# Level masks on GpSimd alone, the first loads spread over three queues, and one gate column later in the fill

## The chip, the cores and the metric

One core of a Trainium2 chip runs the kernel. Its engines are TensorE (PE in the profile, with its weight loads as PEld), VectorE (DVE), ScalarE (ACT), GpSimd (POOL) and SyncE (SP); each works through its own instructions in order. SP, ACT and POOL can also issue DMAs. The metric is the device time of one execution in microseconds; lower is better.

## The reference

One decoder block on a sequence of 1024 tokens and 1024 channels, all float32:

```
xn   = rms_norm(x, norm1_g);  proj = xn @ w_in          # 1024 x 5632
q_sb k_sb v_sb | q_hg f_hg i_hg g_hg | gate_sb gate_hg = split(proj)
o_sb = stick_breaking(rms_norm(q), rms_norm(k), v)      # 8 heads of 64, strictly causal
o_hg = hgrn2(q_hg, f_hg, i_hg, g_hg, lb, hg_norm_g)     # 4 heads of 128: gated linear recurrence
mixed = sigmoid(gate_sb) * (o_sb @ w_b1) + sigmoid(gate_hg) * (o_hg @ w_b2)
h    = x + mixed @ w_out
out  = h + (silu(hn @ w_gate) * (hn @ w_up)) @ w_down,  hn = rms_norm(h, norm2_g)
```

Stick breaking needs, for each query, a reverse running sum of softplus over the keys. HGRN2 needs products of decays between any two tokens of a chunk of 128; the kernel splits these by levels (64, 32, ..., 1), and at each level a mask picks the pairs of tokens that belong to it.

## The kernel before, in words

Activations lie channel by token: a tile has 128 channels and 512 or 1024 tokens, and the tokens are worked in two halves h = 0 and 1. Every float32 product is three matmuls on float32r parts: a number is rounded to its high part (hi, ah, oh, th) and the rest (lo, al, ol, tl) is subtracted out, and hi·hi, hi·lo and lo·hi are summed. One matmul has 128 rows and 512 columns.

**Prologue.** Ahead of the plan, `hybrid_block` issues the load of `vec` (norm gains and lower-bound table, tile `vt`) on SP (line 245), the first halves of the first two weight columns (q and k of head pair 0, tiles `kb`, 256 KB each) on ACT (lines 353 to 357), builds constants on DVE and POOL (`setup`, lines 288 to 315; lines 301 to 315 need `vt`), and lets TensorE run `WARM` = 9 matmuls on ones (line 374).

**The plan.** Everything after it is collected by `Plan.op` with a modelled duration, a rank and its dependencies, and `Plan.issue` (line 140) then simulates the engines and emits the instructions in the order of that simulation. So each engine's order is fixed when the program is built. Ties go by stage, then rank, then longest path. Buffers come from rings of fixed size (`RINGS`, line 384); an instruction that opens a buffer isn't emitted until one is free. Planned instructions all carry line 203.

**Stage one** (to about 665 us): `take_x` (line 547) loads the eight 128-channel tiles of x for each half, rounds them with the norm gain (ACT writes `ah`, DVE `al`), and adds up squares (`tail`). `proj` (line 584) makes one 128-channel column of the projection for one half: 8 × 3 matmuls into a PSUM bank `pj` (3 banks). The columns come in the order `fill_cols` and then `FILL` (line 30): capital G is a gate column, a small a is q, k and v of the next head pair, g, i, f, q are the HGRN2 columns. These matmuls have rank -1: they fill TensorE between the attention and HGRN2 matmuls. `take` (line 634) works up each column; for q, k and v it leaves PSUM by DVE (`aa<-pj`, `vx<-pj`). `scores` makes score blocks `z` (2 banks), `values` transposes v (`ms<-ident,vx`) and forms the outputs, `hgrn` (line 757) does the recurrence. A weight column is loaded by SP as one 512 KB tile `w`, rounded by GpSimd (`split_w`, `pool_copy`, tile `oh`, ring of 4) and subtracted by DVE (`ol`).

`level_masks` (line 509) makes the seven int8 masks `mk`. For each level GpSimd writes a 128-column pattern into a borrowed `tmp` tile (ring of 2) with one memset and two affine selects, and DVE copies it out in four pieces in the order even blocks, odd blocks, so that `hgrn`'s `copy_predicated` (line 807) can read the mask as one run of 256 bytes (`packed`).

```
                  V(nc.vector.tensor_copy, mask[:, e, a].rearrange("p (n m) -> p n m", m=m), src,
                V(nc.vector.copy_predicated, late(at, m), packed(lvl_mask[li], m), packed(lv, m),
```

**Later stages**: branch product (to 0.86 ms), output product, SwiGLU FFN and down product with Strassen-Winograd sums; the change doesn't touch them.

Of the kernel before, what the change touches and what calls it, by code (L numbers as in the profile page):

```python
# [26 lines left out]
EPS = 1e-6  # L27
NEG = -float(2.0**100)
LEVELS = [64, 32, 16, 8, 4, 2, 1]
FILL = ["GgGGaifq", "gGaGfiqGG", "gaGGGiqGfGG", "gGGG"]  # L30
BANKS = [3, 2, 3]
WARM = 9
ORDER = [1, 6, 2, 5, 7, 4, 3]
DOWN = [1, 6, 2, 7, 5, 4, 3]

# [188 lines left out]
def hybrid_block(ctx: ExitStack, tc, xT, wi, wb, wo, wg, wu, wd, vec, outT):  # L224
# [17 lines left out]
        return bank("ms", BANKS[2])  # L242

    vt = const.tile([P, V_W], F32, name="vt")
    nc.sync.dma_start(vt, vec)

    def load_w(src, pool=None):
        t = (pool or wpool).tile([P, 1024], F32, tag="w", bufs=2, name="w32")
# [101 lines left out]
    st1 = ExitStack()  # L350
    hgp = st1.enter_context(tc.tile_pool(name="hgp", bufs=1, reuse_waits="tile"))

    first_w = []
    for n, v in fill_cols[:2]:
        t = hgp.tile([P, HALF], F32, tag="kb", bufs=4, name="kb")
        nc.scalar.dma_start(t, wi[COL[n] + v][:, :HALF])
        first_w.append(t)
    nc.scalar.preload_act_table_set("natural_log_exp_and_others")
    pre = ExitStack()
    pp = pre.enter_context(tc.tile_pool(name="prep", bufs=1))  # L360
# [100 lines left out]
    def G(fn, *args, us, rank=0, after=(), holds=(), **kw):  # L461
        return plan.op("G", us, [(fn, args, kw)], rank, after, holds=holds)
# [46 lines left out]
    def level_masks():  # L509

        for m in LEVELS:
            mk = const1.tile([P, 2, 2, 64], I8, name=f"mk{m}")
            one = new("tmp").bitcast(I8)[:, :P].rearrange("p (n m) -> p n m", m=m)
            G(nc.gpsimd.memset, one, 1.0, us=0.1, after=(last_split[0],))
            G(nc.gpsimd.affine_select, out=one, in_=one, pattern=[[-m, P // m], [0, m]],
              compare_op=ALU.is_ge, fill=0.0, base=0, channel_multiplier=1, us=0.4)
            G(nc.gpsimd.affine_select, out=one, in_=one, pattern=[[m, P // m], [0, m]],
              compare_op=ALU.is_ge, fill=0.0, base=m - 1, channel_multiplier=-1, us=0.4)
            mask = fixed(mk)
            for e in range(2):  # L520
                src = one.rearrange("p (n e) m -> p e n m", e=2)[:, e]
                for a in range(2):
                    V(nc.vector.tensor_copy, mask[:, e, a].rearrange("p (n m) -> p n m", m=m), src,
                      n=64, part=True)
            lvl_mask.append(mask.bitcast(U8).rearrange("p e a t -> p (e a t)"))


    xh = [[fixed(xn[k][0]) for h in range(2)] for k in range(KT)]
# [4 lines left out]
    def load(dst, src, kb, rank=1):  # L533
        last_load[0] = L(dst, src, kb, rank=rank, after=(last_load[0],))

    def split_w(src):
        hi, lo = new("oh", dt=F32R), new("ol", dt=F32R)
        last_split[0] = pool_copy(hi, src, rank=1, after=(last_split[0],))
        V(tt, lo, src, hi.bitcast(F32), op=ALU.subtract, rank=1)
        return hi, lo  # L540

    def take_w(col):
        w = new("w", (P, 1024))
        load(w, wi[col], 512)
        return [split_w(w[:, 512 * i:512 * i + 512]) for i in range(2)]

    def take_x(h):
        ss, acc, ws, sqs = new("ms"), new("tail"), [[], []], []
        if h == 0:
            plan.ring("kb", 4)  # L550
            for u in range(2):
                w = Buf("kb", lambda u=u: first_w[u])
                hi, lo = new("oh", dt=F32R), new("ol", dt=F32R)
                plan.at[A(nc.scalar.copy, hi, w, rank=3)] = 2.4 + 0.6 * u
                V(tt, lo, w, hi.bitcast(F32), op=ALU.subtract, rank=2)
                ws[u].append((hi, lo))
        for k in range(KT):
            x = new("aa" if h == 0 else ("xf", "xq", "xi", "xg")[k // 2])
            load(x, xT[k][:, hs(h)], 256)
            if h == 0 and k in (2, 3):  # L560
                u = k - 2
                n, v = fill[u]
                w = new("kb")
                load(w, wi[COL[n] + v][:, HALF:], 256)
                ws[u].append(split_w(w))
# [12 lines left out]
        M(2048, [(ss, ones, acc, True, True)])  # L578
        rstd(rr[h], ss, D, rank=1 - h)
        return ws  # L580
# [3 lines left out]
    def proj(ws, h, after=None):  # L584

        pss = [new("pj") for _ in ws]
        for k in range(KT):
            cols = slice(k % 4 * P, (k % 4 + 1) * P)
            for ps, w in zip(pss, ws):
                hi, lo = w[k // 4]  # L590
                last_fill[0] = M(1536, [
                    (ps, hi[:, cols], xh[k][h][:, hs(h)], k == 0, False),
                    (ps, hi[:, cols], xl[k][h][:, hs(h)], False, False),
                    (ps, lo[:, cols], xh[k][h][:, hs(h)], False, k == KT - 1)],
                    rank=-1, after=(last_fill[0], after))
            after = None
        return pss

# [158 lines left out]
    def hgrn(hd, last):  # L757
# [14 lines left out]
        for h in range(2):  # L772
# [12 lines left out]
            for li, m in enumerate(LEVELS):  # L785
                dl, lv = new("dl"), new("ms")
                if m == 1:
                    ev = packed(dl, 1)
                    V(tt, ev, late(bb, 1), early(bb, 1), op=ALU.subtract, n=256)
                    A(act, dl[:, :256], dl[:, :256], AF.Exp, n=256)  # L790
                    for t in (early(key, 1), late(q, 1)):
                        V(tt, ev, ev, t, op=ALU.mult, n=256)
                    last = sums(lv[:, :256], dl[:, :256], ones_r, 256, (last,))
                else:


                    dk, dq, rb = mixed(dl, m), packed(dl, m, 256), edge(bb, m)
                    V(tt, dk, rb, early(bb, m), op=ALU.subtract, n=256)
                    V(tt, dq, late(bb, m), rb, op=ALU.subtract, n=256, part=True)
                    A(act, dl, dl, AF.Exp)  # L800
                    V(tt, dq, late(q, m), dq, op=ALU.mult, n=256)
                    V(tt, dk, dk, early(key, m), op=ALU.mult, n=256)
                    cols = lambda t, k: t.strided(k, (P, 2), (1, 64))
                    last = M(0, [(cols(lv, 64 * a), dl[:, a * P:a * P + P],
                                  cols(dl, 256 + 64 * a), True, True) for a in range(2)],
                             after=(last,), us=0.44)
                V(nc.vector.copy_predicated, late(at, m), packed(lvl_mask[li], m), packed(lv, m),
                  n=256)
            kd, ktok, qe, bl = new("tail"), new("tail"), new("tail"), new("bl", (P, 4))
            V(tt, four(kd), bb.strided(P - 1, (P + 1, 2), (P, 2), (0, P)), four(bb),  # L810
# [458 lines left out]
```

## Time and profile before

| what | value |
| --- | --- |
| median of three runs | 1499.47 us (1499.05 to 1499.71) |
| profiled execution: own time, span | 1500.49 us, 1498.8 us |
| PE busy | 1482.0 us (99%) |
| DVE busy | 1199.5 us (80%) |
| ACT busy | 803.4 us (54%) |
| POOL busy | 111.8 us (7%) |

The profile is of one execution. Its span runs from the first to the last instruction of the program; 1.7 us of its own time lie outside. Busy PE is modelled: matmuls are pipelined, and one row shows a matmul as 0.39 us long though the next starts 0.23 us later. So stretches in which PE waits are read from starts and from the idle time in brackets. Times in rows are counted from the start of the span.

### The profile page before, as it was taken

The page shows a single profiled execution, that of the slowest core. Times are in us where ns is not written, and L with a number is a line of the kernel's source. Part 1 is how long each engine was busy: PE and PEld are TensorE (multiplying, and loading weights), DVE is VectorE, ACT ScalarE, POOL GpSimd, SP SyncE. Part 2 cuts the span into 40 slices and gives each one's busy share as a digit, 9 for nine tenths or more (in the row PEclk, how much of TensorE's full clock was granted, in tenths as well). Part 3 has the DMA queues.
Part 4 walks back from the last instruction along what each step waited for, and adds up shares of the span by engine and source line. Part 5 has one row for each costly group of instructions (what it writes and reads, how often), then busy time and mean ns, then how long its engine had stood idle before and what let it go on. Part 6 is the DMA issues. An engine that isn't in the chain of part 4 may idle for free.

```text
span 1498.8 us, 20171 instructions
## 1 busy us (share of the span) xinstructions
PE 1482.0 (99%) x7021; PEld 1224.4 (82%) x7021; DVE 1199.5 (80%) x2130; ACT 803.4 (54%) x1505; POOL 111.8 (7%) x160
## 2 busy tenths in 40 slices
PE   8999999999999999999999999999999999999999
PEld 6788888888888888888888888888888888788887
DVE  9899788988899776977867798888888888575553
ACT  7776878768858877545334453333333333354442
POOL 3311110111112001100000000000000000000000
PEclk9999999999999999999999999999999999999999
DMA  5111111111111121126434344445444444797672
GB/s 183 42 41 60 64 34 47 43 47 60 44 63 47 55 57 60 61 99 254 155 112 146 114 153 173 164 164 160 165 168 168 169 169 171 267 319 227 196 220 89
DMA packets 83157, 188.50 MB, mean 126 GB/s; under 512 B 9584, under 2 KB 11632, under 8 KB 83056
## 3 DMA queue, kind: packets, MB, share of 16 engines
q1 hardware_dynamic: 72400, 167.82, 33.8%
q10 hardware_dynamic: 10656, 19.40, 3.6%
q8 instruction: 55, 0.90, 0.3%
q14 instruction: 46, 0.38, 0.1%
HBM read 131.61 MB, written 55.57 MB: 125 GB/s over the span
## 4 chain that ended last, share of the span: by engine, by line
PE 71%; DVE 11%; ACT 4%; issue 2%; DMA 1%; POOL 0%; ACTq 0%; DVEq 0%; POOLq 0%; SPq 0%
PE pj L203 30%; PE ms L203 16%; PE f L1177 13%; PE z L203 12%; DVE dl L203 2%; DVE aa L203 2%; ACT aa L203 2%; DVE kb L203 2%; DVE ol L203 1%; DVE tl L203 1%; DVE ww L203 1%; ACT ww L203 1%; ACT tmp L203 0%; ACT qhh L203 0%; DMA hb<-h_d 0%
## 5 line engine op out<-in xcount | busy, mean ns | idle before, releaser
L203 PE MATMUL pj<-ah,oh 128*128 128x512 f32 x704 | 286.9, 408 | 1.3 <-DVE aa L203 0.9
L203 PE MATMUL pj<-al,oh 128*128 128x512 f32 x704 | 275.7, 392 | 1.2 <-DVE al L203 1.2
L203 PE MATMUL pj<-ah,ol 128*128 128x512 f32 x704 | 276.2, 392 | 0.0
L203 ACT CAST oh<-w 128x512 fp32r<-128x512 f32 x164 | 99.6, 620 | 242.3 <-PE ms L203 83.7
L203 DVE TENSOR_TENSOR ol<-w,oh 128x512 fp32r<-128x512 f32 x248 | 170.7, 692 | 15.7 <-POOL oh L203 10.4
L203 PE MATMUL ms<-f,oh 128*128 128x512 f32 x528 | 162.7, 389 | 0.2 <-DVE g L203 0.2
L203 PEld LDWEIGHTS pj<-ah,ol 128*128 128x128 f32 x704 | 132.3, 188 | 29.2
L203 PEld LDWEIGHTS pj<-al,oh 128*128 128x128 f32 x704 | 132.9, 189 | 24.9 <-DVE al L203 3.0
L203 PEld LDWEIGHTS pj<-ah,oh 128*128 128x128 f32 x704 | 132.7, 189 | 24.0 <-DVE aa L203 1.4
L203 PEld LDWEIGHTS ms<-f,oh 128*128 128x128 f32 x528 | 99.0, 188 | 21.3 <-DVE g L203 0.6
L1177 PE MATMUL f<-bl,ah 128*128 128x512 f32 x296 | 115.4, 390 | 0.4 <-DVE bl L257 0.2
L1177 PE MATMUL f<-bh,ah 128*128 128x512 f32 x296 | 115.3, 389 | 0.3 <-ACT bh L256 0.3
L1177 PE MATMUL f<-bh,al 128*128 128x512 f32 x296 | 115.2, 389 | 0.0
L203 PE MATMUL pj<-f,oh 128*128 128x512 f32 x352 | 108.3, 389 | 0.0
L203 PE MATMUL z<-f,oh 128*128 128x512 f32 x352 | 108.3, 389 | 0.0
L203 DVE TENSOR_TENSOR_SCAN aa<-aa,ww 128x512 f32<-128x512 f32 (+3 forms) x96 | 92.6, 980 | 18.9 <-ACT aa L203 13.7
L257 DVE TENSOR_TENSOR al<-ra,ah 128x512 fp32r<-128x512 f32 x73 | 50.4, 691 | 70.4 <-ACT ah L256 70.2
L203 PE MATMUL ms<-f,ol 128*128 128x512 f32 x264 | 102.7, 389 | 0.0
L256 ACT CAST ah<-ra 128x512 fp32r<-128x512 f32 x73 | 45.5, 624 | 95.9 <-PE f L1177 87.5
L203 POOL TENSOR_SCALAR oh<-w 128x512 fp32r<-128x512 f32 x84 | 65.3, 777 | 413.2 <-PE pj L203 319.4
L203 PE MATMUL pj<-mx,oh 128*128 128x512 f32 x256 | 78.8, 389 | 0.0
L203 PEld LDWEIGHTS z<-f,oh 128*128 128x128 f32 x352 | 66.1, 188 | 13.7
(257 smaller groups left out, 3136.4 us busy)
## 6 DMA issues: line engine op xcount, KB each, us to landing
w<-wi SPq DMA_DIRECT2D x42, 512.0 KB, 3.7
rb<-act_d SPq DMA_DIRECT2D x73, 256.0 KB, 4.1
w<-wg SPq DMA_DIRECT2D x22, 512.0 KB, 3.6
w<-wu SPq DMA_DIRECT2D x22, 512.0 KB, 3.9
w<-wd SPq DMA_DIRECT2D x22, 512.0 KB, 4.6
wd_d<-ds SPq DMA_DIRECT2D x44, 256.0 KB, 3.0
ra<-wd_d SPq DMA_DIRECT2D x44, 256.0 KB, 4.0
act_d<-c SPq DMA_DIRECT2D x40, 256.0 KB, 4.6
```

Of the source, the lines that this page charges most:

```text
L203: fn(*[a.real() if isinstance(a, View) else a for a in args], **{k: v.real() if isinstance(v, View) else v for k, v in kw.items()})
L256: pin(nc.scalar.copy(hi, src))
L257: pin(nc.vector.tensor_tensor(lo, src, hi.bitcast(F32), op=ALU.subtract))
L1177: nc.tensor.matmul(banks[SET[o]][d], l[:, ws], r, start=start and i == 0, stop=p == NP - 1 and i == 2, skip_group_check=True)
```

## The change

The level masks are made by GpSimd alone: one memset and four affine selects a level on a tile of 256 columns, with no DVE copies and no `tmp`. The mask now repeats the 128-column pattern, and `copy_predicated` reads it by `mixed`, in strides (runs of m bytes), instead of in one run. `vec` is loaded by GpSimd's queue. x's first tile is the first DMA on SP's queue; the two first weight tiles come in pieces of 256 columns (128 KB): the first piece of each on ACT's queue, the second on SP's queue after the second x tile. The first pieces are rounded by DVE, the second by ACT. For the first two columns the order of the three matmuls is hi·ah, lo·ah, hi·al, and at the first x tile the four matmuls on `ah` of both columns stand before the two on `al`. `proj` holds the first weight tile of a column until the column's last matmul. `WARM` is 8. In `FILL`, the third gate column of the first string moves from fourth place to the end.

```diff
-FILL = ["GgGGaifq", "gGaGfiqGG", "gaGGGiqGfGG", "gGGG"]
+FILL = ["GgGaifqG", "gGaGfiqGG", "gaGGGiqGfGG", "gGGG"]
-WARM = 9
+WARM = 8
-    nc.sync.dma_start(vt, vec)
+    nc.gpsimd.dma_start(vt, vec)
-        nc.scalar.dma_start(t, wi[COL[n] + v][:, :HALF])
+    first_w = [(t[:, :256], t[:, 256:]) for t in first_w]
+    nc.scalar.dma_start(first_w[0][0], first_src[0][:, :256])
+    nc.scalar.dma_start(first_w[1][0], first_src[1][:, :256])
...
-            mk = const1.tile([P, 2, 2, 64], I8, name=f"mk{m}")
-            one = new("tmp").bitcast(I8)[:, :P].rearrange("p (n m) -> p n m", m=m)
-            G(nc.gpsimd.memset, one, 1.0, us=0.1, after=(last_split[0],))
...
-                for a in range(2):
-                    V(nc.vector.tensor_copy, mask[:, e, a].rearrange("p (n m) -> p n m", m=m), src,
-                      n=64, part=True)
+            mk = const1.tile([P, 2 * P], I8, name=f"mk{m}")
+            G(nc.gpsimd.memset, mask, 1.0, us=0.15, after=(last_split[0],))
+            for a in range(2):
+                part = mask[:, a * P:(a + 1) * P].rearrange("p (n m) -> p n m", m=m)
+                G(nc.gpsimd.affine_select, out=part, in_=part, pattern=[[-m, P // m], [0, m]],
+                  compare_op=ALU.is_ge, fill=0.0, base=0, channel_multiplier=1, us=0.5)
+                G(nc.gpsimd.affine_select, out=part, in_=part, pattern=[[m, P // m], [0, m]],
+                  compare_op=ALU.is_ge, fill=0.0, base=m - 1, channel_multiplier=-1, us=0.5)
...
+    def first_piece(pieces, u, i):
+        cut, src = slice(256 * i, 256 * i + 256), fixed(first_w[u][i])
+        if i:
+            load(src, first_src[u][:, cut], 128)
+            hi, lo = (Buf(None, lambda b=b: b.buf.tile) for b in pieces[0])
+            op = A(nc.scalar.copy, hi[:, cut], src, n=256, rank=2, holds=pieces[0])
+        else:
+            hi, lo = new("oh", dt=F32R), new("ol", dt=F32R)
+            op = V(nc.vector.tensor_copy, hi[:, cut], src, n=128, rank=3)
+            plan.at[op] = 2.6 + 0.6 * u
+        V(tt, lo[:, cut], src, hi[:, cut].bitcast(F32), op=ALU.subtract, n=256, rank=3 - i)
+        pieces.append((hi, lo))
...
+                mms = [(ps, hi[:, cols], xh[k][h][:, hs(h)]), (ps, hi[:, cols], xl[k][h][:, hs(h)]),
+                       (ps, lo[:, cols], xh[k][h][:, hs(h)])]
+                if len(ws) > 1:
+                    mms[1:] = mms[:0:-1]
...
+            if len(ws) > 1 and k == 0:
+                a, b = groups
+                groups = [a[:2] + b[:2], a[2:] + b[2:]]
+            for mms in groups:
+                last_fill[0] = M(512 * len(mms), mms, rank=-1, after=(last_fill[0], after),
+                                 holds=[v for w in ws for v in w[0]])
...
-                V(nc.vector.copy_predicated, late(at, m), packed(lvl_mask[li], m), packed(lv, m),
+                V(nc.vector.copy_predicated, late(at, m), mixed(lvl_mask[li], m), packed(lv, m),
```

## Rows read from the trace of the kernel before

**Rows 1.** Engines by stretch: start:end length, each engine's busy us (instructions), PE clock, DMA.
```profile
20.00:40.00 20.00, 18.15 (x71) 12.76 (x72) 20.00 (x38) 13.46 (x24) 7.66 (x12) 1.00 0.19 54
...
160.00:665.00 505.00, 500.35 (x2642) 418.35 (x2642) 429.38 (x826) 374.62 (x766) 70.08 (x93) 1.00 0.17 52
665.00:1498.80 833.80, 829.21 (x3652) 684.70 (x3650) 623.43 (x994) 311.94 (x510) 2.02 (x2) 1.00 0.53 179
```
**Rows 2.** PE waits, whole program: waiter, releaser, us in total, times, longest.
```profile
PE ms L203 <- DVE kb L203: 1.6, 6, 0.4
```
**Rows 3.** Timeline, all engines, first 6 us: start, length, engine, operation, [idle before, releaser].
```profile
0.79 0.90 ACTq L356 DMA_DIRECT2D kb<-wi  x2
...
0.80 0.38 SPq L245 DMA_DIRECT2D vt<-vec  x1
...
1.23 1.37 SPq L203 DMA_DIRECT2D aa<-xT  x3
...
2.98 0.15 DVE L301 TENSOR_SCALAR qg<-vt 128x1 f32<-128x1 f32 x1 [0.97 <-DMA vt<-vec]
...
4.49 0.17 DVE L314 TENSOR_SCALAR omlb<-lb 128x4 f32<-128x4 f32 x1
...
5.23 0.72 ACT L203 ACTIVATE ah<-aa,vt 128x512 fp32r<-128x512 f32 x1 [0.87 <-DMA aa<-xT]
```
**Rows 4.** Timeline of PE, 1 to 9 us.
```profile
1.43 4.21 PE L375 MATMUL ms<-ones_r 128*128 128x512 f32 x9 [1.43 <-DVE ones_r L362]
6.00 0.50 PE L203 MATMUL pj<-ah,oh 128*128 128x512 f32 x1 [0.36 <-ACT ah L203]
6.79 0.50 PE L203 MATMUL pj<-al,oh 128*128 128x512 f32 x1 [0.29 <-DVE al L203]
...
8.80 0.50 PE L203 MATMUL pj<-al,oh 128*128 128x512 f32 x1 [0.29 <-DVE al L203]
```
**Rows 5.** Timeline of DVE and PE around 50 us.
```profile
48.06 1.74 DVE L203 COPY mk<-tmp 128x64 int8<-128x64 int8 x3 [1.41 <-POOL tmp L203]
...
55.21 0.75 DVE L203 TENSOR_TENSOR vx<-pj,rr 128x256 f32<-128x256 f32 x2
```
```profile
55.77 0.68 PE L203 MATMUL ms<-ident,vx 128*128 128x128 f32 x4 [2.19 <-ACT aa L203]
```
**Rows 6.** Engines by stretch, right after that wait.
```profile
56.00:58.00 2.00, 2.00 (x9) 1.64 (x8) 1.64 (x8) 1.92 (x7) 0.00 (x0) 0.69 0.43 172
58.00:60.00 2.00, 2.00 (x7) 1.43 (x6) 2.00 (x6) 1.45 (x4) 0.00 (x0) 0.50 0.00 0
```
**Rows 7.** Tile tmp to 70 us: duration ns min/median/max, first and last start us, form.
```profile
L203 DVE COPY mk<-tmp x28: 180/189/1184, 16.0 to 56.3; 128x64 int8<-128x64 int8 x28
L203 POOL TENSOR_SCALAR_AFFINE_SELECT tmp<-tmp x14: 397/732/1198, 11.1 to 49.8; 128x128 int8<-128x128 int8 x14
L203 POOL MEMSET tmp<- x7: 199/204/490, 10.8 to 47.2; 128x128 int8 x7
```
**Rows 8.** Timeline of POOL and DVE, 11 and 34 us.
```profile
11.10 2.54 POOL L203 TENSOR_SCALAR_AFFINE_SELECT tmp<-tmp 128x128 int8<-128x128 int8 x4
```
```profile
33.72 1.10 DVE L203 TENSOR_TENSOR tl<-aa,th 128x512 fp32r<-128x512 f32 x1
```
**Rows 9.** The page's costliest groups: busy us, mean ns | idle before.
```profile
L203 DVE TENSOR_TENSOR ol<-w,oh 128x512 fp32r<-128x512 f32 x248 | 170.7, 692 | 15.7 <-POOL oh L203 10.4
...
L203 POOL TENSOR_SCALAR oh<-w 128x512 fp32r<-128x512 f32 x84 | 65.3, 777 | 413.2 <-PE pj L203 319.4
```
**Rows 10.** Tile mk: its masked copies, and two of them on the timeline of DVE.
```profile
L203 DVE COPY_PREDICATED kb<-mk,ms x56: 421/444/747, 96.5 to 659.0; 128x256 f32<-128x256 uint8 x56
```
```profile
138.33 1.58 DVE L203 COPY_PREDICATED kb<-mk,ms 128x256 f32<-128x256 uint8 x2
```
**Rows 11.** Timeline of PE and DVE: first half of the first head's scores ends; q1 leaves PSUM.
```profile
107.24 0.39 PE L203 MATMUL z<-khl,qlz 128*128 128x512 f32 x1
```
```profile
170.28 0.67 DVE L203 TENSOR_TENSOR aa<-pj,rr 128x512 f32<-128x512 f32 x1
```

More of the change, by code (lines that the diff above doesn't have):

```diff
@@ L351, in hybrid_block @@
     hgp = st1.enter_context(tc.tile_pool(name="hgp", bufs=1, reuse_waits="tile"))
-    first_w = []
-    for n, v in fill_cols[:2]:
-        t = hgp.tile([P, HALF], F32, tag="kb", bufs=4, name="kb")
-        nc.scalar.dma_start(t, wi[COL[n] + v][:, :HALF])
-        first_w.append(t)
+    first_w = [hgp.tile([P, HALF], F32, tag="kb", bufs=4, name="kb") for _ in range(2)]
+    first_w = [(t[:, :256], t[:, 256:]) for t in first_w]
+    first_src = [wi[COL[n] + v] for n, v in fill_cols[:2]]
+    nc.scalar.dma_start(first_w[0][0], first_src[0][:, :256])
+    nc.scalar.dma_start(first_w[1][0], first_src[1][:, :256])
     nc.scalar.preload_act_table_set("natural_log_exp_and_others")
@@ L511, in level_masks @@
         for m in LEVELS:
-            mk = const1.tile([P, 2, 2, 64], I8, name=f"mk{m}")
-            one = new("tmp").bitcast(I8)[:, :P].rearrange("p (n m) -> p n m", m=m)
-            G(nc.gpsimd.memset, one, 1.0, us=0.1, after=(last_split[0],))
[L515 to L518, printed above, removed]
-            mask = fixed(mk)
-            for e in range(2):
-                src = one.rearrange("p (n e) m -> p e n m", e=2)[:, e]
-                for a in range(2):
-                    V(nc.vector.tensor_copy, mask[:, e, a].rearrange("p (n m) -> p n m", m=m), src,
-                      n=64, part=True)
-            lvl_mask.append(mask.bitcast(U8).rearrange("p e a t -> p (e a t)"))
+            mk = const1.tile([P, 2 * P], I8, name=f"mk{m}")
+            mask = fixed(mk)
+            G(nc.gpsimd.memset, mask, 1.0, us=0.15, after=(last_split[0],))
[5 more added lines that the diff above has]
+                  compare_op=ALU.is_ge, fill=0.0, base=m - 1, channel_multiplier=-1, us=0.5)
+            lvl_mask.append(mask.bitcast(U8))
     xh = [[fixed(xn[k][0]) for h in range(2)] for k in range(KT)]
@@ L534, in load, with split_w @@
         last_load[0] = L(dst, src, kb, rank=rank, after=(last_load[0],))
-    def split_w(src):
+    def split_w(src, rank=1):
         hi, lo = new("oh", dt=F32R), new("ol", dt=F32R)
-        last_split[0] = pool_copy(hi, src, rank=1, after=(last_split[0],))
-        V(tt, lo, src, hi.bitcast(F32), op=ALU.subtract, rank=1)
+        last_split[0] = pool_copy(hi, src, rank=rank, after=(last_split[0],))
+        V(tt, lo, src, hi.bitcast(F32), op=ALU.subtract, rank=rank)
         return hi, lo
@@ L549, in take_x @@
         if h == 0:
-            plan.ring("kb", 4)
             for u in range(2):
[L552 to L556, printed above, removed]
+                first_piece(ws[u], u, 0)
         for k in range(KT):
@@ L559, in take_x @@
             load(x, xT[k][:, hs(h)], 256)
+            if h == 0 and k == 1:
+                for u in range(2):
+                    first_piece(ws[u], u, 1)
             if h == 0 and k in (2, 3):
@@ L564, in take_x @@
                 load(w, wi[COL[n] + v][:, HALF:], 256)
-                ws[u].append(split_w(w))
+                ws[u].append(split_w(w, 2))
             g = vt[:, V_N1 + k:V_N1 + k + 1]
@@ L588, in proj @@
             cols = slice(k % 4 * P, (k % 4 + 1) * P)
+            groups = []
             for ps, w in zip(pss, ws):
[L590 to L595, printed above, removed]
+                hi, lo = w[k // 4 if len(w) == 2 else (0, 0, 1, 1, 2, 2, 2, 2)[k]]
+                mms = [(ps, hi[:, cols], xh[k][h][:, hs(h)]), (ps, hi[:, cols], xl[k][h][:, hs(h)]),
+                       (ps, lo[:, cols], xh[k][h][:, hs(h)])]
+                if len(ws) > 1:
+                    mms[1:] = mms[:0:-1]
+                groups.append([(*m, k == i == 0, k == KT - 1 and i == 2)
+                               for i, m in enumerate(mms)])
+            if len(ws) > 1 and k == 0:
[4 more added lines that the diff above has]
+                                 holds=[v for w in ws for v in w[0]])
             after = None
```

## The prediction

> **What bounds the kernel now.** I read the page's busy shares first, then the busy time by stretch, then the waits of PE, then the timeline where these pointed. From 665 us to the end PE starts 3652 matmuls and transposes in 833.80 us, one every 0.23 us, with 4.6 us idle [rows 1]: TensorE is the bound, and nothing there is touched. From 160 to 665 us PE lacks 505 - 500.35 = 4.65 us [rows 1]. The waits lie in the first 60 us. PE's first real matmul starts at 6.00 us, after x's first tile has landed and ACT has rounded it from 5.23 us [rows 3, 4]. Then it waits twice for DVE's `al` [rows 4]. Between 20 and 40 us DVE is busy 20.00 of 20.00 us while PE has 18.15 [rows 1]: there DVE sets the pace. At 55.77 us PE has stood 2.19 us [rows 5], its longest wait after the start. The row names ACT, but the transpose reads `vx`, and DVE begins to write `vx` only at 55.21 us; that is the releaser I believe. After the wait the granted clock reads 0.69 and then 0.50 [rows 6], that is the 1.2 GHz level for most of 4 us. A microsecond saved here is saved at the end, since all that follows is PE's own work.
>
> **The change part by part.**
>
> *Start.* Before, 13.5 KB of vec, two 256 KB weight tiles and 256 KB of x had been asked for ahead of or with x's landing at 5.23 us, 781 KB from an issue at 0.79 us; x's own issue was at 1.23 us, behind vec on SP [rows 3]. Vec took 2.98 - 0.80 = 2.18 us with almost nothing ahead of it; what came after it cost 5.23 - 2.98 = 2.25 us. Now 525 KB are in the way: 2.25 × 525/781 = 1.5, so x lands at about 4.5 us and `ah` is done at 5.2 us (0.72 more). The eight warm-up matmuls end at 1.43 + 4.21 × 8/9 = 5.2 us [rows 4]. The weights are now rounded on DVE behind the small chain that needs vec: it began at 2.98 and ended at 4.49 + 0.17 = 4.66 us, 1.68 us [rows 3]. Two roundings of 256 columns are between a 64-column copy (0.19 us, rows 7) and a 512-column subtraction (0.69 us, rows 9); I take 0.3 us each, so 5.3 us if vec lands when it did. I take 5.3 us for the first matmul, 0.7 us earlier. A load by GpSimd's queue is nowhere in this trace. Bounds: vec's own 2.18 us (the warm-up then allows 0.8 us of gain) and x's 5.23 - 1.23 = 4.0 us, by which vec lands at 4.8 us and PE starts at 4.8 + 1.68 + 0.6 = 7.1 us, 1.1 us later than before. I take the first, as the row of the same bytes. If vec lands after 3.7 us, every 0.1 us goes to the start. POOL's own constants slip behind that issue; what follows them on POOL is the first rounding, which waits for its DMA anyway.
>
> The Trainium skill, DMA: Bandwidth & Descriptors, section on latency and other measured facts, gives about 1 us to the first byte for GpSimd's path and 0.6 us for SP's; no run here shows it yet. By that estimate vec lands 0.4 us later, the start gains 0.3 us instead of 0.7, and the sum below is 0.4 us smaller.
>
> *Order of the first matmuls.* PE waited for `al` with 6.79 - 6.00 = 0.79 us between two starts where 0.23 is normal, 0.56 us lost, and again before 8.80 us with the same idle 0.29 [rows 4]. Now four matmuls on `ah` (0.9 us) stand before the first on `al`, and two instead of one later. The first wait goes, half of the second: -0.8 us. Bounds 0 (if the weights' `lo`, now second, is late instead) and -1.1.
>
> *Masks.* 28 DVE copies of 0.19 us go: 5.3 us of DVE. POOL gets 28 selects for 14, and memsets of 256 columns for 128. All lie off PE's path until the first masked copy near 96 us; what matters is who is behind them. On DVE: everything up to 56 us, and PE lacks 20 - 18.15 = 1.85 us between 20 and 40, so at best -1.85. On POOL: the roundings `oh` of the next weights and `th` of q and k, on which DVE's in-order queue waits. The one side frees DVE, the other can starve it; bounds -1.85 and +5.2 (third rival), taken as 0, since the first four selects took 2.54/4 = 0.64 us [rows 8] and that is about where POOL just keeps up (see there).
>
> *The stall at 55.77 us.* Ahead of `vx`, DVE spent 1.74 us in three mask copies and stood 1.41 us for POOL's `tmp` [rows 5]: 3.15 us that go, more than PE's 2.19. The low clock cost 2 × 0.31 + 2 × 0.50 = 1.6 us [rows 6]; without the wait it should not fall. Together 3.8 us; I leave 0.5 standing for what comes next (DVE's rank of work there is otherwise unchanged): -3.3. Bounds 0 and -3.8.
>
> *Strided masks.* The masked copies take 0.44 us in the median, 0.75 at most; the slow ones are the last two levels of a half (1.58 us for two at 138.33 us) [rows 10], where the written runs are of two and one elements. If runs of 8 and 4 mask bytes did the same, 16 copies would cost 0.30 us more, 4.8 us of DVE; below nothing it can't go, as the old read was one run. PE waited 1.6 us [rows 2] for the output of 56 × 0.44 = 25 us of them, 6%; I take 6% of 4.8, +0.3. Bounds 0 and +4.8.
>
> *Gate column.* 48 matmuls of 0.23 us, 11 us, move behind q1, k1, v1 and three more columns. Nothing is added. q1 needs the first half of head 0's scores, whose last matmul starts at 107.24 us; q1 left PSUM at 170.28 us [rows 11], so without the column it would begin at about 170 - 8 - 11 = 151 us: no new wait. The order of all that follows up to 665 us is drawn anew; the waits there are 4.65 us in 505, so some 1 us either way in the 107 us that the move spans; 0.
>
> Sum: -0.7 - 0.8 + 0 - 3.3 + 0.3 + 0 = -4.5 us. The profiled execution took 1500.49 us (span 1498.8), 1.0 us over the median of the runs, so 1496.0 in its terms and 1495.0 us as a median.
>
> **The rivals.**
>
> *Vec comes late.* The start gains nothing or loses up to 1.1 us: 1495.7 to 1496.8. For it: nothing on DVE or ACT can round before vec. Against: 0.7 us of slack between 2.98 and 3.7.
>
> *The stall only moves.* Removed copies don't help if DVE's place in the order of `vx` moves too, or if another input of the values (a bank of `ms`, the second half of v) is late; then the 3.3 us stay: 1498.3, no change to be told. For it: the named releaser is ACT, not DVE. Against: 3.15 us on DVE right ahead.
>
> *GpSimd becomes the bound ahead of 40 us* (slower). Selects at the median 0.73 us: 28 × 0.73 + 7 × 0.20 = 21.8 us [rows 7] from 10.8 us to 32.6. Then the six roundings that POOL owes by then (four `oh`, two `th`), 6 × 0.78 = 4.7 [rows 9], end at 37.3, and DVE's `tl` behind the last 1.10 us later at 38.4; it ended at 34.8 before [rows 8]. PE's sum for k stands in order behind it: 3.6 us, and a wait of that length costs the clock as above, 1.6. DVE is then later than what it saves at 48 us, so the old stall stays. 1499.5 - 1.5 + 3.6 + 1.6 + 0.3 = 1503.5. It decides from selects over 0.59 us, where `tl` ends as before; the fastest took 0.40, the first four 0.64, the median 0.73. Against: the weights' roundings have the higher rank and overtake masks that haven't begun, and masks aren't needed for another 60 us.
> A subtraction beside POOL's rounding took 1.10 us [rows 8] against 0.69 in the mean [rows 9], so more reads by GpSimd also slow DVE. The Trainium skill, SBUF — State Buffer, section on who interferes with whom, says that a VectorE instruction with two SBUF inputs contends with a GpSimd one that reads SBUF; the trace agrees, and it is why this rival has 0.20 and not less.
>
> **How the numbers follow.** The forecast 0.46, vec late 0.12, the moved stall 0.22, GpSimd the bound 0.20. What a measurement can tell from no change is 0.2%, 3.0 us: under 1496.5 is faster, over 1502.5 slower. Faster: 0.46 and most of vec late, 0.10, give 0.56; same 0.02 + 0.22 = 0.24; slower 0.20. The forecast's own range is 1492.0 to 1496.5 (start, order and 20 to 40 us at their good ends; half the stall left). The whole range goes from 1491.0 (0.07 below, a luckier redrawn order) to 1504.5 (0.11 above, the strided masks or a second stall on top).
>
> **What would show it.** PE's first matmul on `pj` at 5.2 to 5.5 us, and DVE's first read of `vt` before 3.7. No idle before the first matmul on `al`. No `mk` copies on DVE, 28 selects on POOL, their median and where the last one ends: before 31 us is harmless. No PE idle over 1 us between 28 and 60 us and a clock of 1.00 throughout. Masked copies with a median under 0.5 us. The forecast is wrong if the clock falls to 0.50 anywhere before 100 us, if PE starts after 6 us, or if idle time between 100 and 665 us grows by over 2 us.

## The result, and the profile after

| what | before | after |
| --- | --- | --- |
| median | 1499.73 us (6 runs) | 1506.91 us (6 runs, 1505.82 to 1509.28) |
| ratio | | 1.005, interval 1.004 to 1.006 |
| profiled execution: own time, span | 1500.49 us, 1498.8 us | 1505.82 us, 1504.1 us |
| PE's first real matmul | 6.00 us | 6.84 us |
| start of PE's last projection matmul of stage one | 688.99 us | 695.01 us |

The changed kernel is 7.2 us slower; forecast were 4.5 us less. The two profiled executions are 5.3 us apart, and by the last row the changed kernel is 6.0 us behind when stage one's projection ends: the loss is complete there, and what follows takes the same time within 0.7 us.

The stretches of the kernel after, which answer to [rows 1] and [rows 6]:

```profile
8.00:11.00 3.00, 2.90 (x7) 2.32 (x8) 2.97 (x10) 3.00 (x8) 2.34 (x5) 0.51 1.06 397
20.00:40.00 20.00, 14.91 (x56) 9.43 (x54) 17.68 (x24) 9.02 (x16) 18.91 (x22) 0.97 0.09 29
40.00:45.00 5.00, 4.19 (x8) 2.67 (x9) 2.62 (x4) 1.91 (x4) 0.22 (x1) 0.50 0.35 102
160.00:665.00 505.00, 500.13 (x2633) 417.29 (x2632) 432.01 (x827) 375.54 (x769) 74.55 (x92) 1.00 0.17 53
```

The columns after the length are PE, PEld, DVE, ACT and POOL, then the granted clock. From 20 to 40 us PE is busy for 14.91 us (18.15 before) and now it is not DVE (17.68) but POOL (18.91) that has hardly a gap. The granted clock is at the 1.2 GHz level (half clock) twice, from 8 to 11 and from 40 to 45 us. From 160 to 665 us PE's total is as before.

The first 7 us, all engines, answer to [rows 3, 4]:

```profile
1.32 0.70 POOL L245 DMA_DIRECT2D vt<-vec  x1 [0.81 <-POOLq L1268]
1.45 3.59 PE L375 MATMUL ms<-ones_r 128*128 128x512 f32 x8 [1.45 <-DVE ones_r L362]
...
4.12 0.29 DVE L203 CAST oh<-kb 128x256 fp32r<-128x256 f32 x1 [2.08 <-DMA kb<-wi]
...
6.07 0.15 DVE L301 TENSOR_SCALAR qg<-vt 128x1 f32<-128x1 f32 x1 [1.66 <-DMA vt<-vec]
6.07 0.72 ACT L203 ACTIVATE ah<-aa,vt 128x512 fp32r<-128x512 f32 x1 [3.06 <-DMA vt<-vec]
...
6.84 0.50 PE L203 MATMUL pj<-ah,oh 128*128 128x512 f32 x1 [1.81 <-ACT ah L203]
```

DVE and ACT go on at the same 6.07 us, both released by vec's DMA: it took 4.75 us from its issue, against 2.18 from SP's queue before. The trace's DMA records say where: on GpSimd's queue vec's packets run from 4.70 to 5.51 us, so 3.4 of the 4.75 us pass before the first of them; on SP's queue the first ran at 1.80 us, 1.0 us after the issue. DVE's first rounding of a weight (`oh<-kb`, 4.12 us) did not wait for vec. PE has stood 1.81 us since the warm-up, and at 8 us its clock falls. That is this one execution: in the profiles of five more kernels below with vec on GpSimd's queue (e2, e4, e9, e11, e17) PE stands 1.60 to 2.00 us there, and the clock reads 1.00 from 8 to 11 us.

The tile of the masks, which answers to [rows 7] and [rows 10]:

```profile
L203 DVE COPY_PREDICATED kb<-mk,ms x56: 416/444/749, 102.9 to 666.1; 128x256 f32<-128x256 uint8 x56
L203 POOL TENSOR_SCALAR_AFFINE_SELECT mk<-mk x28: 355/725/1580, 10.6 to 34.6; 128x128 int8<-128x128 int8 x28
L203 POOL MEMSET mk<- x7: 304/307/328, 10.1 to 22.2; 128x256 int8 x7
```

The masked copies are as long as before. The 28 selects have the old median and end at 36.17 us. What POOL and PE do meanwhile, on their timelines:

```profile
22.49 9.95 POOL L203 TENSOR_SCALAR_AFFINE_SELECT mk<-mk 128x128 int8<-128x128 int8 x11
32.41 1.20 POOL L203 TENSOR_SCALAR oh<-w 128x512 fp32r<-128x512 f32 x2
33.58 1.05 POOL L203 TENSOR_SCALAR th<-aa 128x512 fp32r<-128x512 f32 x1
34.59 1.58 POOL L203 TENSOR_SCALAR_AFFINE_SELECT mk<-mk 128x128 int8<-128x128 int8 x1
37.26 0.93 POOL L203 TENSOR_SCALAR th<-aa 128x512 fp32r<-128x512 f32 x1 [1.09 <-ACT aa L203]
```
```profile
34.85 0.39 PE L203 MATMUL ms<-th,bones_r 128*128 128x512 f32 x1
37.77 0.50 PE L203 MATMUL ms<-tl,bones_r 128*128 128x512 f32 x1 [2.53 <-DVE tl L203]
...
40.81 2.08 PE L203 MATMUL ms<-tail,ones 128*128 128x512 f32 x2 [1.82 <-DVE tail L203]
41.90 1.42 PE L203 MATMUL ms<-th,bones_r 128*128 128x512 f32 x1
```

27 of the 28 selects stand ahead of the first rounding `oh<-w`. DVE's timeline has the next subtraction waiting for it.

```profile
33.06 2.10 DVE L203 TENSOR_TENSOR ol<-w,oh 128x512 fp32r<-128x512 f32 x2 [2.31 <-POOL oh L203]
...
37.03 0.68 DVE L203 TENSOR_TENSOR tl<-aa,th 128x512 fp32r<-128x512 f32 x1
```

So PE waits 2.53 us for `tl` and 1.82 us for `tail`, and runs at half clock to 45 us. The old stall at 55.77 us [rows 5] is gone: PE has no idle time between 50 and 60 us.

PE's lost time can be counted over the whole of stage one: the time from each start of PE to the next, less the median of that for the kind of instruction (over all traces here), summed. By this count PE loses 15.5 us in the first 60 us (11.9 before), 8.3 from 60 to 160 (6.2), 8.9 from 160 to 300 (6.9) and 22.0 from there to 680 us (23.1). So just over half of the 6.5 us lost anew lies in the first 60 us. The experiments use the same count.

### The profile page after: what moved, and what is told of

Same layout as the page of the kernel before. It is cut to its first block, busy times and chain, and to the rows that moved or that the text cites. A ratio compares the mean times of both kernels' runs of the same rounds, so it can differ in the third digit from the quotient of the medians.

```text
span 1504.1 us, 20190 instructions
## 1 busy us (share of the span) xinstructions
PE 1482.9 (99%) x7020; PEld 1224.8 (81%) x7020; DVE 1199.9 (80%) x2106; ACT 803.2 (53%) x1505; POOL 130.8 (9%) x175
## 4 chain that ended last, share of the span: by engine, by line
PE 82%; DVE 9%; ACT 4%; issue 2%; POOL 2%; DMA 1%; SPq 0%; DVEq 0%; POOLq 0%; ACTq 0%
PE pj L203 36%; PE ms L203 19%; PE f L1194 14%; PE z L203 12%; DVE dl L203 2%; ACT aa L203 2%; POOL mk L203 1%; DVE aa L203 1%; DVE kb L203 1%; DVE ol L203 1%; DMA ld<-o_d 1%; ACT ww L203 1%; DVE tl L203 1%; DVE ww L203 1%; DVE tail L203 1%
## 5 line engine op out<-in xcount | busy, mean ns | idle before, releaser
L203 POOL TENSOR_SCALAR oh<-w 128x512 fp32r<-128x512 f32 x84 | 71.1, 848 | 352.4 <-PE pj L203 291.8
L203 PEld LDWEIGHTS pj<-f,oh 128*128 128x128 f32 x352 | 66.1, 188 | 13.7
```

The source lines that it names most:

```text
L203: fn(*[a.real() if isinstance(a, View) else a for a in args], **{k: v.real() if isinstance(v, View) else v for k, v in kw.items()})
```

## The experiments

The kernel before took 1499.3 to 1499.5 us in the median beside them; ratios are to it, with 95% intervals. "First matmul" is PE's first real one.

### Which term is the loss

**e1_vec_on_sp.** The changed kernel with vec first on SP's queue.

```diff
-    nc.gpsimd.dma_start(vt, vec)
+    nc.sync.dma_start(vt, vec)
```


> The changed kernel (1506.9 us), with one edit: vec is loaded by SP's queue again, ahead of x. Only the prologue's instructions change place; the planned order stays. Theory A (vec by GpSimd's queue landed at 6.07 us and held the first matmul to 6.84 us, and the gap dropped the clock): first matmul at 5.2 to 5.6 us, no half clock at 8 to 11 us, 1.4 + 1.4 us less: 1504. Rival B (GpSimd's mask selects, which don't start sooner for it, pin TensorE at 37 us): what is won at the start is waited for there, 0 to 1 us less: 1506 to 1507.

Measured: 1506.86 us, 1.0048 [1.0031, 1.0065]. PE's timeline:

```profile
5.56 0.50 PE L203 MATMUL pj<-ah,oh 128*128 128x512 f32 x1 [0.56 <-ACT ah L203]
...
34.74 0.49 PE L203 MATMUL ms<-th,bones_r 128*128 128x512 f32 x1 [2.31 <-POOL th L203]
37.83 0.80 PE L203 MATMUL ms<-tl,bones_r 128*128 128x512 f32 x1 [2.59 <-DVE tl L203]
```
PE starts 1.28 us earlier and all of it is gone at 37.8 us: the matmul on `tl` starts at the same time as after. DVE, which is ready earlier too, stands 4.95 us for POOL's `oh` and begins the subtraction at 33.13 us (33.06 after). POOL sets that time, not the start.

**e2_short_selects.** The same instructions in the same order on every engine, each select on 8 columns instead of 128 and with a pattern of one run of 8 in place of the blocks (not shown), so that the masks are not complete.

```diff
-                part = mask[:, a * P:(a + 1) * P].rearrange("p (n m) -> p n m", m=m)
+                part = mask[:, a * P:a * P + 8]
...
```


> The changed kernel, with each of the 28 selects of the masks on 8 columns instead of 128 (the masks are left wrong; every instruction, its place in each engine's order and all modelled costs stay). Theory B (GpSimd is the bound ahead of 40 us: its roundings th and oh stand behind masks until 32.4 us): the waits at 34.85 (2.5 us), 38.56 (1.8) and 41.9 us and the half clock after them go, 6 us less: 1501. Rival C (the order drawn anew by the moved gate column costs the time): 1506 or more. Under both vec's late landing stays.

Measured: 1499.95 us, 1.0006 [0.9997, 1.0015]. The tile of the masks, POOL's timeline, and PE's longest wait from 12 to 60 us:

```profile
L203 POOL TENSOR_SCALAR_AFFINE_SELECT mk<-mk x28: 187/645/1312, 10.9 to 29.9; 128x8 int8<-128x8 int8 x28
```
```profile
21.25 5.53 POOL L203 TENSOR_SCALAR_AFFINE_SELECT mk<-mk 128x8 int8<-128x8 int8 x11
26.75 2.13 POOL L203 TENSOR_SCALAR oh<-w 128x512 fp32r<-128x512 f32 x2
```
```profile
35.68 1.12 PE L203 MATMUL ms<-tail,ones 128*128 128x512 f32 x2 [1.85 <-DVE tail L203]
```
The 28 selects take 16.5 us in all instead of 23.2, and the rounding comes at 26.75 us instead of 32.41. Shorter selects alone give back 7.0 us, and stage one's last projection matmul comes at 688.77 us. The wait for `tl` is gone; that for `tail` stays, but the clock does not fall. So the selects' time is the loss here, not vec, which came as late as after (first matmul at 7.11 us).

Short selects do two things at once. POOL's rounding comes earlier, and DVE is faster in itself: up to its first `tl` the same 42 planned instructions take 28.1 us here and 31.1 us after, beside the longer selects. An estimate of the two: after, DVE stood 2.31 us for the rounding, and without that wait it would have begun the subtraction at 30.75 us, still 2.4 us later than here (28.32). Which share of the 7.0 us belongs to each this run does not separate; in e1 the longer wait of DVE (4.95 us) shows that POOL was the later of the two.

**e3_short_and_vec.** Both edits.

> Both of the former edits: short selects and vec on SP. Theories A and B together: both losses go, 1506.9 - 6 - 2.8 = 1498. If A's loss was hidden behind B's, this shows it against the run with short selects alone: 1501 - 2.8. Rival C: 1504 or more stays, in waits after 60 us.

Measured: 1499.81 us, 1.0006 [0.9997, 1.0015]. By the medians, 0.14 us apart, nothing of the earlier start reaches the end. In the profiled execution the first matmul came at 5.20 us and stage one ended 1.2 us earlier than in e2 (687.54 us); but that execution, at 1503.05 us the slowest of its runs, lost some 4 us at the border of the stages, 690 to 698 us, where PE waits for the next product's `o`, so it doesn't show where the others lost the start.

### The parts without the masks

**e4_gate_back** and **e5_gate_alone.** The gate column back in its old place in the changed kernel; and the moved column alone in the kernel before.

```diff
-FILL = ["GgGaifqG", "gGaGfiqGG", "gaGGGiqGfGG", "gGGG"]
+FILL = ["GgGGaifq", "gGaGfiqGG", "gaGGGiqGfGG", "gGGG"]
```


> The changed kernel, with the gate column back in its old place (FILL as before); the order of stage one after 90 us is drawn anew. Rival C (the moved column costs the 1 us that the lag grows by after 60 us, or more): 1502 to 1506. Theories A and B: 1506 to 1508, as both losses lie before 50 us.

> The kernel before (1499.5 us), with the gate column moved as in the change and nothing else. The kernel with short selects kept 1.2 us more lost time between 60 and 160 us and 2.3 us more between 160 and 300 us than the kernel before. Theory D (the moved column costs these 3.5 us): 1503. Rival E (these come of the order that the other edits drew): 1499 to 1500, and the stall of 2.19 us at 55.77 us stays in either case, as all before 90 us keeps its order.

Measured: e4 1514.03 us, 1.0096 [1.0081, 1.0111]; e5 1503.91 us, 1.003 [1.0018, 1.0042]. Moved in the changed kernel the column is worth -7.1 us, moved alone it costs 4.6. In each of the two slower ones there is one long wait that the other order doesn't have; PE's timeline of e4, then of e5:

```profile
452.60 0.53 PE L203 MATMUL z<-khl,qhh 128*128 128x512 f32 x1 [4.44 <-DVE ww L203]
```
```profile
283.95 0.68 PE L203 MATMUL z<-khl,qhh 128*128 128x512 f32 x1 [1.81 <-DVE ww L203]
```
Both are the same kind: a score block stands in PE's fixed order ahead of projection matmuls, and needs a bank of `z` that DVE hasn't read out. The moved column is stored at 157 and 165 us in e4 and at 244 and 251 us in e5: e4's wait lies 290 us behind it, e5's 33 us. The clock falls behind both (granted 0.66 from 452 to 457 us and 0.57 from 284 to 288).

**e6_masks_alone.** The kernel before with the change's masks and strided reads alone.

> The kernel before, with the masks by GpSimd alone (and read in strides) and nothing else. Theory B: roundings behind masks on GpSimd cost 7 us, the stall at 55.77 us (3.8 with its clock) goes, 1499.5 + 7 - 3.8 = 1502.7, with waits on tl and tail at 32 to 42 us. Rival (masks only harm together with the earlier start and the held weight tiles): 1496 to 1497.

Measured: 1503.26 us, 1.0025 [1.0015, 1.0035]. The old stall is gone, and PE's timeline has a longer one, ahead of which DVE stands 3.15 us for POOL's `oh`:

```profile
32.19 0.79 PE L203 MATMUL pj<-ah,oh 128*128 128x512 f32 x1 [4.74 <-DVE aa L203]
```

**e9_start_alone**, **e10_start_vec_on_sp**, **e11_start_and_gate**, **e13_no_masks_vec_sp.** The change with the masks and their reads as before: e9 and e10 with the gate column as before, e11 and e13 with it moved; e10 and e13 with vec first on SP's queue.

> The changed kernel, with the masks made as before (DVE copies, read in one run) and the gate column back: what is left of the change is the start (vec by GpSimd's queue, x first, pieces of weights, the matmul order, WARM 8, held weight tiles). Theory A (vec lands at about 6 us; first matmul 0.8 to 1.1 us later than before, two waits on al less, -0.8): 1499 to 1500.5. Rival (the held tiles and the new order of matmuls cost by themselves): 1502 or more.

> As the run of the start alone, but with vec on SP's queue. With masks out of GpSimd's way the earlier first matmul (5.2 to 5.6 us) should reach the end: 1.5 us less than the start alone, 1498 to 1499. If DVE, which is busy without a break from 10 to 36 us, sets the pace there: the same as the start alone.

> The changed kernel, with the masks made as before and all else kept. If the parts add up: the start alone plus the 4.6 us of the moved column, about 1504, and the masks are the rest (3) of the 1506.9. If masks cost 7 us here too, as the run with short selects says for the whole change: 1500.

> The whole change without its masks (these as before: one GpSimd mask of 128 columns and four VectorE copies per level), and vec first on SP's queue. The order on every engine is that of e11_start_and_gate (1496.74 us). Theory A, masks and vec's queue are two separate losses: vec's 1.4 to 1.7 us (e1's first matmul, e10 against e9) carry to the end, 1495.0 to 1495.4 us, under the kernel before by 0.3%. Theory B, the earlier start is given back at the next wait, as in e1: 1496.7 us within 0.5.

| kernel | us | ratio | first matmul | stage one's last projection matmul |
| --- | --- | --- | --- | --- |
| e9: start | 1503.61 | 1.0027 [1.0016, 1.0039] | 6.98 | 691.22 |
| e10: start, vec on SP | 1502.24 | 1.0019 [1.001, 1.0028] | 5.51 | 689.56 |
| e11: start, gate | 1496.74 | 0.9985 [0.9976, 0.9995] | 7.22 | 686.93 |
| e13: start, gate, vec on SP | 1495.79 | 0.9977 [0.9967, 0.9986] | 5.28 | 684.81 |

All of the change except its masks is 2.6 us faster than before (e11), so within it the masks cost 10.2 us. By the count 2.2 us of these lie from 300 to 680 us, where the order is another. In the profiled executions vec's queue costs 1.7 and 2.1 us by the end of stage one (e9 to e10, e11 to e13); in the medians it is 1.4 and 0.95 us, each of which the runs alone can't tell from nothing. The start of e13 on the timeline:

```profile
2.92 0.15 DVE L301 TENSOR_SCALAR qg<-vt 128x1 f32<-128x1 f32 x1 [0.89 <-DMA vt<-vec]
...
4.50 0.72 ACT L203 ACTIVATE ah<-aa,vt 128x512 fp32r<-128x512 f32 x1 [0.65 <-DMA aa<-xT]
...
5.28 0.77 PE L203 MATMUL pj<-ah,oh 128*128 128x512 f32 x1
```
That e13 and e11 are fast isn't the start alone: their loss from 300 to 680 us is 19.2 and 19.8 us (23.1 before, 25.8 in e9), that from 60 to 300 us 15.9 and 15.7 (13.1 before). The order drawn anew gives and takes some 3 to 4 us in each.

### Why the roundings stand behind the selects

`Plan.issue` orders POOL's work by modelled durations, 0.15 us for a memset and 0.5 for a select: 7 × (0.15 + 4 × 0.5) = 15.1 us. The trace has 2.2 + 23.2 = 25.4 us. The planner emits in the order of its simulation, so by its model GpSimd had done 27 selects before the first rounding could begin; if the durations are the reason, telling it the true ones must move the roundings ahead.

**e15_true_costs**, **e17_cost_alone**, **e18_before_masks_cost.** Only the numbers that the planner is told: in the changed kernel with vec on SP (beside e1), in the changed kernel itself, and in e6.

```diff
-            G(nc.gpsimd.memset, mask, 1.0, us=0.15, after=(last_split[0],))
+            G(nc.gpsimd.memset, mask, 1.0, us=0.3, after=(last_split[0],))
...
-                  compare_op=ALU.is_ge, fill=0.0, base=0, channel_multiplier=1, us=0.5)
+                  compare_op=ALU.is_ge, fill=0.0, base=0, channel_multiplier=1, us=0.75)
...
-                  compare_op=ALU.is_ge, fill=0.0, base=m - 1, channel_multiplier=-1, us=0.5)
+                  compare_op=ALU.is_ge, fill=0.0, base=m - 1, channel_multiplier=-1, us=0.75)
```


> The changed kernel with vec on SP's queue, and the planner that draws the order told 0.75 us for a select and 0.3 for a memset, in place of 0.5 and 0.15 (both as the trace has them in the median); the instructions are the same, only their order can move. Theory A, the roundings stand behind the selects because the planner took these for shorter than they are: the roundings now come first, 1498 to 1501 us. Rival, the planner put them there whatever they cost, since GpSimd is free when they become ready: 1505 to 1508 us, as e1 (1506.86).

> The changed kernel, vec on GpSimd's queue as it is there, with the planner alone told 0.75 us for a select and 0.3 for a memset. If what e15 showed (1498.67 us, with vec on SP's queue) is the planner's numbers and vec's queue is a loss beside them, as in e11 against e13 (0.95 us) and e9 against e10 (1.4): 1499.6 to 1500.2 us, some 7 us under the change. Rival, e15's gain needs the early vec: over 1503.

> The kernel before with its masks by GpSimd alone, as in e6_masks_alone (1503.26 us), and the planner told 0.75 and 0.3 us. If the planner's numbers are what the masks cost: the wait of PE at 27 to 32 us (4.74 us on DVE's aa) is gone, 1497.5 to 1500 us. Rival, in the old order of the start GpSimd has no free stretch for 28 selects whatever the planner believes: 1502 to 1505 us.

| with the true costs | us | ratio | the same with the old costs | difference |
| --- | --- | --- | --- | --- |
| e15: change, vec on SP | 1498.67 | 0.9996 [0.9987, 1.0005] | e1 1506.86 | -8.2 |
| e17: change | 1500.23 | 1.0004 [0.9995, 1.0013] | after 1506.91 | -6.7 |
| e18: before, masks alone | 1498.36 | 0.9994 [0.9986, 1.0003] | e6 1503.26 | -4.9 |

POOL's timeline of e17, and PE's two longest waits from 12 to 60 us:

```profile
19.65 4.15 POOL L203 TENSOR_SCALAR_AFFINE_SELECT mk<-mk 128x128 int8<-128x128 int8 x5
25.25 0.87 POOL L203 TENSOR_SCALAR oh<-w 128x512 fp32r<-128x512 f32 x1 [1.45 <-PE pj L203]
...
32.40 3.27 POOL L203 TENSOR_SCALAR_AFFINE_SELECT mk<-mk 128x128 int8<-128x128 int8 x4
35.65 1.90 POOL L203 TENSOR_SCALAR oh<-w 128x512 fp32r<-128x512 f32 x2
37.51 7.70 POOL L203 TENSOR_SCALAR_AFFINE_SELECT mk<-mk 128x128 int8<-128x128 int8 x7
```
```profile
PE ms L203 <- ACT aa L203: 0.7, 1, 0.7
PE ms L203 <- POOL th L203: 0.6, 1, 0.6
```
The selects are not shorter here (24.0 us in all), but only 17 of them stand ahead of the first rounding, which comes 7.2 us earlier and finds POOL idle for its buffer; the rest fill in behind. All three pairs agree: selects as long as before cost far less once fewer of them stand ahead of the roundings. PE's order is drawn anew too, so how much of each difference is the roundings alone isn't shown; e2, with an unchanged order, says 7.0 for shorter selects. Nor is all of the masks' cost taken back: e15 is still 2.9 us over e13 and e17 3.5 us over e11, the same kernels with the masks as before.

**e7_wide_selects** and **e8_masks_late.** Two other ways to keep GpSimd free, both with vec on SP: two selects of 256 columns a level (modelled at 0.75 us each) in place of four of 128; and `level_masks` called only at the fourth column, after its weights.

> The changed kernel, with vec on SP's queue, and each level's mask by two selects of 256 columns instead of four of 128 (correct masks, modelled at 0.75 us each and 0.3 for the memset). A select of 8 columns took 0.65 us in the median against 0.73 for 128, so I expect about 0.8 us for 256: 14 x 0.8 + 7 x 0.3 = 13 us of GpSimd, done by 24 us. Theory B: as the run with short selects and vec on SP or better, 1497 to 1500. If selects take time by columns (1.4 us each), 1506.

> The changed kernel, with vec on SP's queue, and the masks added to the plan only after the weights of the first forget column have been split (all 28 selects of 128 columns, behind about 50 us, when GpSimd has long idle stretches; first masked copy near 97 us). Theory B: waits at 32 to 42 us go, 1498 to 1500. Rival (DVE is late there by its own work): waits on tl and tail over 2 us stay, 1503 or more.

Measured: e7 1506.17 us, 1.0044 [1.0029, 1.0059]; e8 1506.47 us, 1.0043 [1.0027, 1.006]. Both missed. In e7 half as many selects took longer each, and so did DVE's work beside them; the tile, DVE's and POOL's timelines:

```profile
L203 POOL TENSOR_SCALAR_AFFINE_SELECT mk<-mk x14: 418/1003/2398, 10.9 to 25.5; 128x256 int8<-128x256 int8 x14
```
```profile
20.49 0.68 DVE L203 TENSOR_TENSOR tail<-tail,ww 128x512 f32<-128x512 f32 x1
...
22.23 2.05 DVE L203 TENSOR_TENSOR tail<-tail,ww 128x512 f32<-128x512 f32 x1
```
```profile
30.83 1.33 POOL L203 TENSOR_SCALAR oh<-w 128x512 fp32r<-128x512 f32 x1 [3.08 <-PE pj L203]
```
Here the selects are done at 27.75 us and the first rounding `oh<-w` finds POOL idle, so the roundings are not behind them: PE waits 2.49 us for DVE's `al` at 25.83 us. Selects that slow DVE are a way of their own to lose the time. In e8 the waits from 32 to 42 us shrink to one of 1.5, but the selects now lie at 33 to 58 us, DVE stands 1.24 us for POOL's `oh` at 51.68 us, PE waits 2.23 us for DVE's `vx` at 53 us, and some 6 us go at the border of the stages.

**e12_one_copy**, **e14_one_copy_gate**, **e16_before_one_copy.** A third way: GpSimd makes 128 columns (two selects modelled at 0.6 us), and DVE copies them out once, 256 columns, with the strided read: in the start with vec on SP and the old gate column, in the changed kernel with vec on SP, and in the kernel before.

```diff
+            V(nc.vector.tensor_copy, mask.rearrange("p (a t) -> p a t", a=2),
+              flat.rearrange("p (o t) -> p o t", o=1).to_broadcast([P, 2, P]), n=256)
```


> As the run of the start with vec on SP's queue, but with masks of a third kind: GpSimd writes 128 columns with two selects (as before), one DVE copy writes them twice side by side (7 copies of 256 bytes for 28 of 64), and the masks are read in strides as in the change. 21 copies less are 4 us of DVE where it is the bound, and GpSimd has no more than before. Theory B: the stall at 55 us gets smaller or goes: 1495 to 1498. Rival (the order drawn anew decides by several us either way): anything from 1495 to 1503.

> The changed kernel with vec on SP's queue and half of GpSimd's mask work: two selects of 128 columns per level and one VectorE copy of 256 in place of four selects. Theory A, GpSimd's 28 selects ahead of the roundings are the loss: 14 selects (10 us of GpSimd instead of 20) leave no wait of PE over 1.5 us between 28 and 45 us, and with 7 copies in place of 28 the old stall at 54 us is gone too: 1493 to 1496 us. Rival, selects of any number ahead of the roundings delay them: a wait on the tl of k at 34 to 42 us stays, 1498 to 1502 us.

> The kernel before with one VectorE copy of 256 columns per level in place of four of 64, and the masked copies reading the strided mask; start and gate column as before. If VectorE's copies ahead of vx are what PE waits for at 55.77 us, 21 copies fewer (some 4 us of VectorE less 7 times the longer copy) take that wait away: 1496 to 1497.5 us. If the stall only moves: 1499 to 1500 us. If the order drawn anew costs more than it gives, as in e12 (1504.09): over 1501.

Measured: e12 1504.09 us, 1.0033 [1.002, 1.0046]; e14 1495.33 us, 0.9975 [0.9965, 0.9985]; e16 1499.49 us, 1.0 [0.9992, 1.0009]. In all three the wait before the transposes of `vx` is about 0.2 us or less, and in none does that show in the time. PE's timeline of e14, and of e16:

```profile
43.12 0.51 PE L203 MATMUL ms<-tl,bones_r 128*128 128x512 f32 x1 [1.14 <-DVE tl L203]
53.60 0.44 PE L203 MATMUL ms<-ident,vx 128*128 128x128 f32 x2 [0.18 <-DVE vx L203]
```
```profile
119.41 1.16 PE L203 MATMUL ms<-xi,tail 128*128 128x128 f32 x8 [1.80 <-DVE tl L203]
```
e14 against e13, which differ in the masks alone: the wait at 53 us is gone, one for `tl` at 43 us has come, and both lose 9.5 us in the first 60. In e16 1.8 us are saved in the first 60 us and 2.3 lost from 60 to 160 us. e14 beats both kernels, by 4.2 and 11.6 us; e13 differs from it by less than the runs can tell.

## Why the prediction was wrong

The third rival, GpSimd as the bound ahead of 40 us, is what happened; it was given 0.20 and 1503.5 us.

*Masks*, taken as 0, is the step that failed first: measured are 7.0 us for the selects' length alone (after against e2) and 10.2 us for the masks within the change (after against e11), both past the upper bound of 5.2. With the selects short, all else of the change comes to +0.5 us (e2 against before), where -4.5 were forecast: the first 60 us gain 1.8 us by the count, 60 to 300 us lose 3.0. The rival's condition, selects over 0.59 us, was met by the row that stood beside it: their median was 732 ns before and 725 after. I took the first four instead (0.64 us) and argued that roundings "overtake masks that haven't begun". They can't: the order on POOL is fixed when the program is built, from durations some 40% under the trace's, and 27 selects were put ahead of the first rounding. The rival's working came near: `tl` at 38.4 us was worked out, 37.7 measured; a wait of 3.6 us, 2.53 + 1.82 measured in two; and the low clock behind them. Part of that is luck: three roundings stood between the 27 selects and `tl`, not six, and DVE needed 33.06 to 37.71 us behind the first of them, not 1.10 us behind the last. It kept the old stall, which went, and took the start as a gain, which it wasn't; what else lies between 1503.5 and 1506.9 us was not separated.

*Start*, -0.7, became +0.84, with half clock from 8 to 11 us beside it: vec landed 4.75 us after its issue, not 2.2, and past the other bound too. The half clock belongs to that one execution (see above). With vec in time the step's numbers were right: in e13, with vec at 2.92 us, x landed at 4.50 (worked out: 4.5) and PE started at 5.28 (5.3). Its chain was not: DVE rounds the first weights without waiting for vec's chain, at 4.12 us after and at 3.08 in e13, so PE followed vec by 0.77 us and not by 2.3, and what set 5.28 us in e13 is x, by `ah`, and the warm-up, both done at 5.22 us. By the estimate from the Trainium skill, DMA: Bandwidth & Descriptors, latency and other measured facts, vec would have come 0.4 us later than on SP's queue; measured were 3.1 (6.07 against 2.98; 0.5 of them by the later issue), and the measurement decides. Most of it passes before the first packet; why isn't shown. The Trainium skill, SBUF — State Buffer, who interferes with whom, names VectorE holding a shared port as a way to delay such a load; the trace speaks against it as the main cause, since DVE idles for 2.08 + 1.66 of the 4.75 us. In the change this term was hidden behind the masks (e1: nothing back); without them it is 1.7 to 2.1 us at the end of stage one.

*Order of the first matmuls*, -0.8: the waits for `al` at the start are gone, as forecast, but waits for the weights' `ol` have come for them (0.29 us at 8.10 us after, 0.39 at 6.91 in e13). That is the case of the step's bound 0. From the first matmul on `pj` to the seventh the traces show 2.04 to 3.09 us in the old order and 2.06 to 3.13 in the new, so no gain.

*The stall at 55.77 us*, -3.3: the releaser was read rightly, since DVE's copies gone, the wait is gone (after, e6, e14, e16), and it is back in e8, where DVE is late there for another reason. The 1.6 us for the clock did not belong to the stall: e5, whose order is that of before up to some 90 us, has the same wait (2.21 us at 56.08 us), and its clock reads 1.00 from 56 to 60 us. The term is 0 to -0.5 in the time, neither of which can be told from nothing (e16 against before 0.0; e14 against e13 -0.5): "the stall only moves" was the better case. The 0.5 us left standing for what comes next was too little; `tl` at 43 us and a wait at 119 us came next.

*Strided masks*, +0.3: 0. The median is 444 ns against 444; the strides made no difference that the trace shows.

*Gate column*, 0 ± 1, failed in size: +4.6 alone, -6.9 with the start (e9 to e11), -7.1 in the change (e4 to after). The reasoning looked at the place that moves. What it costs lies behind that, by 33 us in e5 and 290 in e4, where the redrawn order puts a score block ahead of its free bank.

That the sum of terms, 1495.0, is near e14's 1495.33 is chance: the terms that make up e14 are others.

## What to carry to other kernels

Where a planner writes each engine's order from modelled durations, a new kind of instruction must be given the trace's duration first: here the model was short by 0.25 us on each of 28 small selects, and giving it two true numbers took back 5 to 8 us in three pairs of kernels, with the same instructions in another order. Work that nobody waits for soon isn't free on an in-order queue; look at what stands behind it there, not at when its result is needed. And parts of a change that each redraw the order don't add up (moving the gate column was worth +4.6 or -7): cost them together, or change one at a time.

## What the runs showed of the hardware

- A select's time grows far less than its columns: median 0.65 us for 8 (e2, in a simpler pattern), 0.73 for 128 and 1.0 for 256 columns (e7) of int8, with single ones from 0.19 to 2.4.
- DVE slows beside GpSimd's selects, more so beside wider ones: its addition of 512 columns took 0.68 to 0.70 us beside selects of 8 columns (e2), up to 1.09 beside those of 128 (after) and up to 2.06 beside those of 256 (e7).
- A load of 13.5 KB by GpSimd's queue at the start took 4.7 to 5.1 us from its issue to its first reader in six traces; by SP's, 2.0 to 2.5 in fourteen. After, 3.4 of the 4.75 us passed before its first packet.
- A wait of PE of some 2 us lowers the granted clock in some executions and not in others. It read 0.51 from 8 to 11 us after 1.81 us and 0.50 from 40 to 45 us after 2.53 and 1.82 us (both after), but 1.00 after 2.00 us at 7.22 us (e11), 1.85 at 35.68 (e2) and 2.21 at 56.08 (e5).
